# A hybrid diffusion backbone on one core: layer 1's attention-gate round of modulation weights moves to the last heads of layer 1, and modulation steps take two blocks of rows

## The chip, the cores and the metric

The kernel runs on one core of a Trainium2 chip. The metric is the device time of one execution in microseconds (us). Before the change three runs gave 1723.59, 1725.94 and 1725.95 us; the median is 1725.94 us. The engines named below are PE (TensorE, which multiplies matrices), DVE (VectorE), ACT (ScalarE), POOL (GpSimd) and SP (SyncE, which here issues the DMAs).

## The reference, cut to what matters

A two-layer transformer over 512 latent tokens and 256 context tokens, width 1024, all in fp32. Each layer is an attention part and a SwiGLU part, and each part is normalised, modulated, mixed, normalised again and added through a gate. Shift, scale and gate come from the conditioning vectors through one weight matrix per layer, `ada_w[l]` of 1024 x 6144:

```
mx = (silu(c) @ ada_w[l] + ada_b[l])         # 6 chunks of 1024; mc the same from c_ctx
hx = modulate(rmsnorm(x, g0), mx[0], mx[1])  # shift, scale of attention
yx = attention(hx, hc)                       # layer 0: window heads A and differential heads B; layer 1: MLA, 16 heads
x  = x + mx[2] * rmsnorm(yx, g1)             # gate of attention
hx = modulate(rmsnorm(x, g2), mx[3], mx[4])  # shift, scale of SwiGLU
x  = x + mx[5] * rmsnorm(swiglu(hx), g3)     # gate of SwiGLU
```

`ada_w` is 24 MB a layer and each of its elements is used once for two vectors, so it is a stream of loads with a few narrow matmuls behind each.

## The kernel before, in words

The kernel is written as one program for all engines. A scheduler places each engine's instructions in the order in which the code issues them, within what priorities and buffers allow; `tc.issue_after(x)` adds an order edge on PE alone. All DMAs are issued by SP on one queue (q1), in SP's order: a DMA whose buffer is not free yet holds up all DMAs behind it. Most products are made as three matmuls on a high and a low half of each operand, split by ACT (`wh`, `pth`) and DVE (`wl`, `ptl`, line 127).

**Modulation.** `ada_round(l, r, bank, sbt, ring)` (lines 252 to 286) is a Python generator that makes two of the six chunks of layer l: round r = 0 gives shift and scale of attention, r = 1 the gate of attention and the shift of SwiGLU, r = 2 the scale and the gate of SwiGLU. A round goes over 8 blocks of 128 rows. Each block issues two loads of 512 KB (`load`, line 204, tile `wst`, from `in_ada_w`) and, for each load, four matmuls at line 259 into the PSUM tile `ada`. Four matmuls of one load are called a **quad** here. The program's order lists a quad as `x4`; the trace counts two records for each fp32 matmul, so that there a quad is `x8`. After the eighth block the round copies the sums (line 265), transposes them (line 268, four of them), and adds and scales them on DVE (lines 273 to 286). Before the change the generator hands back control after each block, so a round is nine steps: eight blocks and the end. Whoever drives the generator decides where the next step stands in the order of PE; the loads go ahead as soon as the ring of `wst` buffers has a free one.

**Where the rounds stand.** Layer 0's rounds 0 and 1 come early, round 1 among the projections of queries and values (lines 557 to 571). In the differential heads (B, lines 856 to 892) one generator runs layer 0's round 2, then layer 1's rounds 0 and 1. The tables `FIRST` (head 0) and `ORDER` (heads 1 to 3) set at which point of a head each step stands: a letter `a` is one step, `f` transposes, `v` multiplies with values, and the bar splits what goes before and after a tile's softmax. The loads have a ring of 3 buffers, and of 4 once head 0 is two tiles in (`wst_a`). Rounds left over at the end of head 3 would be run out at `steps(ada, 99)`.

**Layer 1's heads** (M, lines 1545 to 1655): 16 heads, `HeadM`, each with scores (`scm`, line 1589), softmax (`p`, line 625), transposes (`tp`, line 639) and values (`pvm`, line 1607). The table `MORE` sets what else each head carries: `k` and `q` project the next pair's keys and queries and move them into place by DMA (`K<-K`, `K<-KR`, `Q<-Q`, `Q<-RQ`, line 133), `r` rotates, `u` makes values, `a` is one modulation step. Before the change heads 13, 14 and 15 carry three `a` each, all of layer 1's round 2, with the 3 buffers of the common ring `stage`. The attention gate of layer 1 is first used after the heads, in `out_proj(1)`.

Of the kernel before, what the change touches and what calls it, by code (L numbers as in the profile page):

```python
# [9 lines left out]
F32 = mybir.dt.float32  # L10
# [8 lines left out]
P = 128  # L19
# [96 lines left out]
def build(tc, d, cat, wat):  # L116
# [3 lines left out]
    def pool(stack, name, bufs=1, side="left", **kw):  # L120
        return stack.enter_context(tc.tile_pool(name=name, bufs=bufs, side=side, reuse_waits="tile", **kw))

    def psum(stack, name, side="left"):
        return stack.enter_context(tc.tile_pool(name=name, bufs=1, side=side, space=PSUM, reuse_waits="tile"))

    def sub(out, a, hi):
        nc.vector.tensor_sub(out, a, hi.bitcast(F32))  # L127
# [12 lines left out]
    wst = pool(top, "wst")  # L140
# [61 lines left out]
    def load(src, width, ring=None):  # L202
        st = (ring or stage).tile([P, 1024], F32, tag="wst", name="wst")
        nc.sync.dma_start(st[:, 0:width], src)
        return st[:, 0:width]
# [11 lines left out]
    def packed(name, ring=None):  # L217
        off, width = wat[name]
        return load(d["wpk"][off:off + P * width].rearrange("(p w) -> p w", p=P), width, ring)
# [32 lines left out]
    def ada_round(l, r, bank, sbt, ring=None):  # L252
        acc = bank()
        for k in range(NK):
            st = [load(d["ada_w"][l, k * P:(k + 1) * P, 2048 * r + 1024 * h:2048 * r + 1024 * h + 1024], 1024, ring)
                  for h in range(2)]
            for h in range(2):
                for q in range(4):
                    nc.tensor.matmul(acc[32 * q:32 * q + 32, 256 * h:256 * h + 256], scst[:, k, :],  # L259
                                     st[h][:, 256 * q:256 * q + 256],  # L260
                                     start=(k == 0 and h == 0), stop=(k == NK - 1 and h == 1),
                                     tile_position=(0, 32 * q), skip_group_check=True)
            yield
        sb = sbt()
        nc.vector.tensor_copy(sb, acc)
        tp = bank()
        for b in range(4):
            nc.tensor.transpose(tp[:, P * b:P * b + P], sb[:, P * b:P * b + P], ident)
        src = tp.rearrange("p (h e q r) -> p h q e r", h=2, e=2, q=4)
        dst = mods[l][:, 16 * r:16 * r + 16, :].rearrange("p (h q e) s -> p h q e s", h=2, q=4)  # L270
        bias = adab[:, l, 16 * r:16 * r + 16].rearrange("p (h q e) -> p h q e", h=2, q=4)
        for h in range(2):
            nc.vector.tensor_add(dst[:, h], src[:, h, :, :, 0:2], bias[:, h].unsqueeze(3).to_broadcast([P, 4, 2, 2]))

        def mk(out, chunk, gi, one):
            g = ng[:, l, gi, :].unsqueeze(2).to_broadcast([P, NK, 2])
            nc.vector.scalar_tensor_tensor(out, mods[l][:, 8 * chunk:8 * chunk + 8, :], one, g,
                                           op0=ALU.add, op1=ALU.mult)
        if r == 0:
            mk(amod[l][0], 1, 0, 1.0)  # L280
        elif r == 1:
            mk(ggc[l][0], 2, 1, 0.0)
        else:
            mk(amod[l][1], 4, 2, 1.0)
            mk(ggc[l][1], 5, 3, 0.0)
        yield

    def steps(gen, n):
        for _ in range(n):
            if next(gen, gen) is gen:  # L290
                break
# [136 lines left out]
    def blocks(name, scale=None):  # L428

        st = packed(name)  # L430
        w = st.shape[1] // 2
        res = []
        for j in range(2):
            h, l = (wring.tile([P, 512], F32R, tag=x, name=x)[:, 0:w] for x in ("wh", "wl"))
            a = st[:, w * j:w * j + w]
            if scale:
                nc.scalar.mul(h, a, scale)
                nc.vector.scalar_tensor_tensor(l, a, scale, h.bitcast(F32), op0=ALU.mult, op1=ALU.subtract)
            else:
                nc.scalar.copy(h, a)  # L440
                sub(l, a, h)
            res.append((h, l))
        return res
# [95 lines left out]
    def queries(i, w=None):  # L539
        big = yield from feat(w or blocks(f"q{i}", 0.125))  # L540
        rope(big[:, 0:NX], QO[:, i, 0:NX], tabs, 16, shift_tile())
        nc.scalar.copy(QO[:, i, NX:NT], big[:, NX:NT])

    def tok(t, src, slabs, width, n=NK):
# [7 lines left out]
        return lambda ps: mm3(lambda k: (src[0][:, k, P * t:P * t + P], src[1][:, k, P * t:P * t + P]), [(ps, mov)], n)  # L552

    ada = ada_round(0, 1, lambda: ps1.tile([P, 512], F32, tag="nt", name="ada"), shift_tile, ring_x)
    steps(keys(0, first[0]), 99)
    steps(queries(0, first[1]), 99)
    for i in range(1, 4):
        with tc.issue_after(ada_end):
            steps(ada, 1)
            steps(queries(i), 99)  # L560
    acc = [b[:, c:c + 384] for b in (bigs.tile([P, 1024], F32, tag="big", name="vps") for _ in range(2)) for c in (0, 512)]
    acc += [ps1.tile([P, 512], F32, tag="sm", name="vps")[:, 0:384] for _ in range(2)]
    for k in range(NK):
        steps(ada, 1)
        if k % 2 == 0:
            va = blocks(f"va{k // 2}")
        for t in range(6):
            for i, (a, b) in enumerate(((0, 0), (0, 1), (1, 0))):
                nc.tensor.matmul(acc[t], hT[a][:, k, P * t:P * t + P], va[k % 2][b],  # L569
                                 start=(k == 0 and i == 0), stop=(k == NK - 1 and i == 2))  # L570
# [285 lines left out]
    ps2 = PS2({"tp": (pstp, 2), "pv": (pst, 1), "ada": (pst, 1)})  # L856
    ptr = Ring((pb, 4))
    COMB = ((0, 1, 3), (3,))
    FIRST = ('v|t', 'w|a a', '|a', 'f0 a|f1 v0 f2', 'a|v1 a', 'a|a v2')
    ORDER = ("f3 a|f4 v3", "f5 v4|v5 a", "f6 a|v6 s", "f0 a|f1 v0", "|f2 v1 a", "|v2 a n")  # L860
    LAST = "f3 f4 v3 f5 v4 f6 v5 v6 s n"

    def run(word, new, old):
        for w in word.split():
            if w == "a":
                last = next(i for i in reversed(nc.cur_bb.bb.instructions) if i.engine == mybir.EngineType.PE)
                with tc.issue_after(last):
                    steps(ada, 1)
            elif w in "vtw":
                run_a(w, None, old)  # L870
            elif w == "s":
                old.squares()
            elif w == "n":
                old.norm(4, 6)
                old.norm(0, 4)
            else:
                x = new if w[1] in "012" else old
                (x.flip if w[0] == "f" else x.values)(int(w[1]))

    ring_a = Ring((wst, 3))  # L880
    ada = (x for l, r in ((0, 2), (1, 0), (1, 1))
           for x in ada_round(l, r, lambda: ps2.tile([P, 512], F32, tag="ada", name="ada"),
                              lambda: ring_a.slots[0][0].tile([P, 512], F32, tag="adasb", name="adasb", bufs=1), ring_a))
    qs = [stack(4, m, qring) for m in range(2)]
    for h in range(4):
        g = HeadB(h, qs)
        for t in range(6):
            a, b = (ORDER if h else FIRST)[t].split("|")
            g.scores(t, lambda: run(a, g, prev))
# [194 lines left out]
    class FfnWide:  # L1084
# [27 lines left out]
        def bank(self, tag):  # L1112

            return next(self.banks[tag]).tile([P, 512], F32, tag="b", name=tag)
# [329 lines left out]
    k = krT[:, 0:NX]  # L1444
# [25 lines left out]
    s_ma = ExitStack()  # L1470
# [74 lines left out]
    vp = pool(s_ma, "v1", bufs=2, side="right")  # L1545
    pp1 = pool(s_ma, "pp1", bufs=6, side="right")
    pt1 = pool(s_ma, "pt1", bufs=3, side="right")
    psb = PS(psum(s_ma, "ps_n"), {"sc": 2, "pv": 1, "tp": 2, "ada": 1})

    def mla_values(g):  # L1550
# [22 lines left out]
    def next_queries(p):  # L1573
        Q = yield from mla_queries(p, wp, psb.tile([P, 512], F32, tag="ada", name="qnps"), RQs[p // 2])
        KQ[p].append(Q)
        yield

    class HeadM:
# [21 lines left out]
        def values(self, j):  # L1600
# [15 lines left out]
    FIRST_M = "S0 u u S1 u u S2 u u f0 S3 x f1 x v0 f2 x v1"  # L1616
    LAST_M = "f3' v2' f4' v3' f5' v4' v5'"
    MORE = ("kkqqquu", "rrruuuu", "kkqqq", "rrr", "kkqqq", "uuuu", "kkqqq", "uurrr", "kkqqq", "uuuu", "kkqqq", "uu",
            "kkqqq", "aaa", "aaa", "aaa")
    V, RQs = {}, {0: RQ}  # L1620

    def chain(gens):
        for g in gens:
            yield from g
# [3 lines left out]
        "r": chain(next_rope(g) for g in range(1, 4)),  # L1628
        "k": chain(next_keys(p) for p in range(1, 8)),
        "q": chain(next_queries(p) for p in range(1, 8)),  # L1630
        "a": ada_round(1, 2, lambda: psb.tile([P, 512], F32, tag="ada", name="ada"), scratch),
    }
    prev = None

# [82 lines left out]
```

## Time and profile before

| what | value |
|---|---|
| median of three runs | 1725.94 us |
| the profiled execution | 1721.91 us, of which the span is 1720.1 us |
| granted TensorE clock, mean of the profiled execution | 0.983 of full speed (2.4 GHz) |
| busy share of the span | PE 95%, DVE 64%, ACT 51%, POOL 24% |
| heads B of layer 0 touched by the change | about 332 to 394 us |
| heads M that carry `a` | about 1237 to 1282 us; the last head ends about 1305 us |

The profile is one execution on the chip. Its page lists busy time of each engine, the span in 40 slices, the chain of work that ended last, and the costliest groups of instructions. The trace behind it can be asked for stretches (busy time of each engine, granted clock, share of DMA time), for waits, and for the instructions one after the other. An idle time is followed by `<-` and by what ended it.

### The profile page before, as it was taken

To read this page: it belongs to the slowest core of one execution; us is meant where nothing else is said; L and a number is where in the kernel's file an instruction comes from. 1 tells how busy PE (TensorE), PEld (TensorE's weight loads), DVE (VectorE), ACT (ScalarE), POOL (GpSimd) and SP (SyncE) were. 2 spreads that over 40 slices of the span, in tenths; PEclk is the share of its full clock that TensorE was granted. 3 is DMA by queue.
4 is the path that set the end of the run, shared out by engine and by line. 5 is a ranking of instruction groups with operands and counts; after the bars stand their busy time and mean duration, and the time that the engine had idled before them with its cause. 6 is when DMAs were issued, how large, how long until landed. Compare 5 with 4: busy or idle time off the path is not lost.

```text
span 1720.1 us, 27699 instructions
## 1 busy us (share of the span) xinstructions
PE 1630.9 (95%) x10274; PEld 1450.1 (84%) x10274; DVE 1095.1 (64%) x1924; ACT 882.8 (51%) x1888; POOL 420.9 (24%) x459
## 2 busy tenths in 40 slices
PE   6899999898979999999999997999999999999998
PEld 4688887667869999999888786899877899999886
DVE  3536888655676555555534866798766778777433
ACT  5325666554654444444333854676655745555332
POOL 2302434551212122221200112232220323332000
PEclk9999999999989999999999998999999999999999
DMA  9531214983323222222523432323463422333322
GB/s 361 188 110 36 63 46 132 258 282 125 109 75 99 72 66 72 98 74 74 210 97 135 163 125 66 81 61 94 101 196 115 144 97 101 99 114 105 102 98 86
DMA packets 61431, 203.35 MB, mean 118 GB/s; under 512 B 7280, under 2 KB 10480, under 8 KB 61296
## 3 DMA queue, kind: packets, MB, share of 16 engines
q1 hardware_dynamic: 61296, 201.58, 37.3%
q8 instruction: 81, 1.33, 0.3%
q14 instruction: 54, 0.44, 0.1%
HBM read 174.29 MB, written 10.49 MB: 107 GB/s over the span
## 4 chain that ended last, share of the span: by engine, by line
PE 79%; DMA 6%; DVE 6%; ACT 4%; issue 2%; POOL 1%; SPq 0%; DVEq 0%; POOLq 0%; ACTq 0%
PE A L1109 15%; PE y L1269 14%; PE C L1109 8%; PE y L230 6%; PE fps L230 6%; DMA wst<-in_ada_w 5%; PE B L1109 4%; PE scm L1589 3%; PE yc L1269 2%; PE tp L639 2%; PE pvm L1607 2%; PE vps L230 2%; PE ada L259 2%; PE vps L569 2%; DVE wl L127 1%
## 5 line engine op out<-in xcount | busy, mean ns | idle before, releaser
L127 DVE TENSOR_TENSOR wl<-wst,wh 128x512 fp32r<-128x512 f32 (+2 forms) x329 | 250.2, 768 | 201.5 <-ACT wh L1101 161.3
L1109 PE MATMUL A<-T,wh 128*128 128x384 f32 (+1 forms) x1280 | 278.9, 310 | 10.2 <-ACT T L936 7.8
L1101 ACT CAST wh<-wst 128x512 fp32r<-128x512 f32 (+1 forms) x266 | 161.8, 617 | 227.6 <-PE y L1269 120.5
L1109 PEld LDWEIGHTS A<-T,wh 128*128 128x128 f32 x1280 | 215.8, 191 | 11.8 <-ACT T L936 8.1
L1109 PE MATMUL A<-T,wl 128*128 128x384 f32 (+1 forms) x640 | 194.7, 310 | 1.0 <-DVE wl L127 1.0
L130 POOL TENSOR_SCALAR p<-p,sum 128x768 f32<-128x768 f32 (+2 forms) x96 | 83.4, 870 | 273.5 <-DVE sum L631 238.7
L1109 PE MATMUL C<-T,wh 128*128 128x384 f32 (+1 forms) x656 | 146.1, 312 | 2.4 <-ACT wh L1101 2.4
L1269 PE MATMUL y<-wl,ah 128*128 128x512 f32 x336 | 130.7, 389 | 0.0
L1269 PE MATMUL y<-wh,ah 128*128 128x512 f32 x336 | 130.4, 389 | 0.0
L1269 PE MATMUL y<-wh,al 128*128 128x512 f32 x336 | 130.4, 389 | 0.0
L1145 POOL TENSOR_TENSOR s<-wst 128x512 f32<-128x512 f32 x42 | 72.2, 1719 | 228.7 <-DMA wst<-in_wpk 167.0
L1101 ACT CAST wh<-S 128x512 fp32r<-128x512 f32 x126 | 73.3, 587 | 101.9 <-PE A L1109 48.5
L1109 PEld LDWEIGHTS A<-T,wl 128*128 128x128 f32 x640 | 121.3, 191 | 1.6 <-DVE wl L127 1.6
L1213 POOL TENSOR_TENSOR g<-g,E 128x384 f32<-128x384 f32 (+1 forms) x63 | 70.0, 1111 | 180.7 <-DVE E L1212 166.8
L1109 PEld LDWEIGHTS C<-T,wh 128*128 128x128 f32 x656 | 111.2, 191 | 2.9 <-ACT wh L1101 2.9
L230 PE MATMUL fps<-hT,wh 128*128 128x512 f32 (+1 forms) x416 | 98.0, 356 | 6.1 <-DVE KS L127 2.9
L1109 PE MATMUL C<-T,wl 128*128 128x384 f32 (+1 forms) x328 | 102.4, 312 | 0.1
L127 DVE TENSOR_TENSOR wl<-S,wh 128x512 fp32r<-128x512 f32 x126 | 85.8, 685 | 21.2 <-ACT wh L1101 20.4
L127 DVE TENSOR_TENSOR ptl<-tp,pth 128x512 fp32r<-128x512 f32 x124 | 84.3, 686 | 17.5 <-ACT pth L642 16.7
L642 ACT CAST pth<-tp 128x512 fp32r<-128x512 f32 x124 | 71.6, 585 | 38.2 <-PE tp L639 33.4
L1589 PE MATMUL scm<-K,Q 96*128 96x512 f32 (+1 forms) x384 | 83.1, 350 | 2.3 <-ACT p L625 1.3
L230 PEld LDWEIGHTS fps<-hT,wh 128*128 128x128 f32 x416 | 65.4, 194 | 19.8 <-PE sc L617 3.6
(390 smaller groups left out, 3985.1 us busy)
## 6 DMA issues: line engine op xcount, KB each, us to landing
wst<-in_wpk SPq DMA_DIRECT2D x107, 512.0 KB, 3.6
wst<-in_ada_w SPq DMA_DIRECT2D x96, 512.0 KB, 5.8
wst<-in_ffn_w SPq DMA_DIRECT2D x66, 512.0 KB, 3.5
xd<-xt SPq DMA_DIRECT2D x14, 512.0 KB, 2.6
xt<-xd SPq DMA_DIRECT2D x14, 512.0 KB, 5.1
xt<-in_x SPq DMA_DIRECT2D x8, 512.0 KB, 4.2
wst<-in_ab_w_out SPq DMA_DIRECT2D x8, 512.0 KB, 4.6
wst<-in_mla_w_out SPq DMA_DIRECT2D x8, 512.0 KB, 4.5
```

What stands on the lines that cost most here:

```text
L127: nc.vector.tensor_sub(out, a, hi.bitcast(F32))
L130: nc.gpsimd.tensor_scalar(out, a, s, 1.0, op0=ALU.mult, op1=ALU.mult)
L230: nc.tensor.matmul(ps, s, mov(k)[m], start=(k == 0 and i == 0), stop=(k == n - 1 and i == 2))
L259: nc.tensor.matmul(acc[32 * q:32 * q + 32, 256 * h:256 * h + 256], scst[:, k, :], st[h][:, 256 * q:256 * q + 256], start=(k == 0 and h == ...
L569: nc.tensor.matmul(acc[t], hT[a][:, k, P * t:P * t + P], va[k % 2][b], start=(k == 0 and i == 0), stop=(k == NK - 1 and i == 2))
L642: nc.scalar.copy(h, tp[:, 0:P * n])
L1101: nc.scalar.copy(h, src)
L1109: nc.tensor.matmul(ps, x, self.T.at(m, i, k), start=(start and k == 0 and j == 0), stop=(stop and k == 3 and j == 2), skip_group_check=True)
L1145: nc.gpsimd.tensor_sub(s3, a11, a21)
L1213: nc.gpsimd.tensor_mul(o, o, e)
L1269: nc.tensor.matmul(ys[t][j], a[x][:, P * place[t]:P * place[t] + P], w[j][y], start=(k == 0 and i == 0), stop=(k == NF - 1 and i == 2))
L1589: nc.tensor.matmul(ps[:, k0:k1], Q[0:96, e, a, P * i:P * i + P], K[0:96, e, b, k0:k1], start=(n == 0), stop=(n == 2))
```

## The change

It does four things.

1. `ada_round` hands back control after each second block: a round is four steps of two blocks (four quads, eight when nothing stands between) and one for the end.
2. In layer 0's round 1 the calls are fewer to match.
3. In the B heads round (1, 1) is dropped from the generator, and `FIRST` and `ORDER` have fewer `a`.
4. In the M heads the generator runs rounds (1, 1) and (1, 2), in ten steps (`aaaa`, `aaa`, `aaa`), with a ring of its own, `ring_m`: the 3 common buffers and 4 new ones (`wst_m`).

```diff
@@ ada_round
-            yield
+            if k % 2:
+                yield
@@ layer 0, round 1
     for i in range(1, 4):
         with tc.issue_after(ada_end):
-            steps(ada, 1)
+            if i > 1:
+                steps(ada, 1)
             steps(queries(i), 99)
...
     for k in range(NK):
-        steps(ada, 1)
         if k % 2 == 0:
+            if k:
+                steps(ada, 1)
             va = blocks(f"va{k // 2}")
@@ B heads
-    FIRST = ('v|t', 'w|a a', '|a', 'f0 a|f1 v0 f2', 'a|v1 a', 'a|a v2')
-    ORDER = ("f3 a|f4 v3", "f5 v4|v5 a", "f6 a|v6 s", "f0 a|f1 v0", "|f2 v1 a", "|v2 a n")
+    FIRST = ('v|t', 'w|a', '|', 'f0 a|f1 v0 f2', '|v1 a', '|a v2')
+    ORDER = ("f3|f4 v3", "f5 v4|v5 a", "f6|v6 s", "f0|f1 v0", "|f2 v1 a", "|v2 n")
...
-    ada = (x for l, r in ((0, 2), (1, 0), (1, 1))
+    ada = (x for l, r in ((0, 2), (1, 0))
@@ M heads
+    ring_m = Ring((wst, 3), (pool(s_ma, "wst_m", side="right"), 4))
...
-            "kkqqq", "aaa", "aaa", "aaa")
+            "kkqqq", "aaaa", "aaa", "aaa")
...
-        "a": ada_round(1, 2, lambda: psb.tile([P, 512], F32, tag="ada", name="ada"), scratch),
+        "a": chain(ada_round(1, r, lambda: psb.tile([P, 512], F32, tag="ada", name="ada"), scratch, ring_m) for r in (1, 2)),
```

How the instructions stand is seen in the order of an engine. PE, at the end of B head 2 and the start of head 3 (`sc<-KS` scores, `pvb` values, `rb` a small transpose of the norm, `tp` transposes of probabilities), before:

```order
L616 MATMUL sc_1315<-KS_470,qb 128x256
L617 MATMUL sc_1315<-KS_470,qb 128x256
L259 MATMUL ada<-wst,scst 32x256 x16
L616 MATMUL sc_1314<-KS_471,qa 128x512
L617 MATMUL sc_1314<-KS_471,qa 128x512
L616 MATMUL sc_1314<-KS_471,qa 128x256
L617 MATMUL sc_1314<-KS_471,qa 128x256
L639 MATMUL tp<-ident,p 128x128 x4
L794 MATMUL pvb<-pth,VB_467 128x256
```

and in the changed kernel at the same place:

```order
L619 MATMUL sc_1315<-KS_470,qb 128x256
L620 MATMUL sc_1315<-KS_470,qb 128x256
L642 MATMUL tp<-ident,p 128x128 x4
L619 MATMUL sc_1314<-KS_471,qa 128x512
L620 MATMUL sc_1314<-KS_471,qa 128x512
L619 MATMUL sc_1314<-KS_471,qa 128x256
L620 MATMUL sc_1314<-KS_471,qa 128x256
L642 MATMUL tp<-ident,p 128x128 x4
L797 MATMUL pvb<-pth,VB_467 128x256
```

The four quads between two scores are gone and the transposes follow the scores directly. From head 1's end to the end of head 3 PE has 28 quads in 23 pieces before; after, 12 in 5 pieces, and one set of four transposes less.

PE in the M heads, where two heads' work overlaps (`scm` scores, `pvm` values, `tp` transposes), before:

```order
L1607 MATMUL pvm<-ptl,V 128x256 x2
L639 MATMUL tp<-ident,p 128x128 x4
L259 MATMUL ada<-wst,scst 32x256 x6
L1589 MATMUL scm<-K,Q 128x512
L1589 MATMUL scm<-K,Q 128x256
L1589 MATMUL scm<-K,Q 128x512
L1589 MATMUL scm<-K,Q 128x256
L1589 MATMUL scm<-K,Q 128x512
L1589 MATMUL scm<-K,Q 128x256
L259 MATMUL ada<-wst,scst 32x256
L639 MATMUL tp<-ident,p 128x128 x4
L259 MATMUL ada<-wst,scst 32x256 x3
```

and in the changed kernel:

```order
L1611 MATMUL pvm<-ptl,V 128x256 x2
L642 MATMUL tp<-ident,p 128x128 x4
L259 MATMUL ada<-wst,scst 32x256 x8
L642 MATMUL tp<-ident,p 128x128 x4
L259 MATMUL ada<-wst,scst 32x256 x4
L1593 MATMUL scm<-K,Q 128x512
L1593 MATMUL scm<-K,Q 128x256
L1593 MATMUL scm<-K,Q 128x512
L1593 MATMUL scm<-K,Q 128x256
L1593 MATMUL scm<-K,Q 128x512
L1593 MATMUL scm<-K,Q 128x256
L259 MATMUL ada<-wst,scst 32x256 x4
```

The quads stand closer together: 32 of them in 27 pieces over heads 13 to 15, where there were 16 in 15 pieces, and two sets of transposes, the second of which stands with the end of head 15.

SP at the start of the M heads (`wst<-in_wpk` weights of keys and queries, `K` and `Q` the moves of the second pair's context part into place):

```order
 L133 DMA Q<-RQ 32x1024 x2
+L204 DMA wst<-in_ada_w 128x1024
 L204 DMA wst<-in_wpk 128x512
 L204 DMA wst<-in_wpk 128x384
+L133 DMA K<-K 64x2x256
 L204 DMA wst<-in_wpk 128x256
-L133 DMA K<-K 64x2x256
+L204 DMA wst<-in_ada_w 128x1024 x3
 L133 DMA K<-KR 32x2x256 x2
```

Four of the moved loads are issued here, some 160 us before the heads that use them, three of them directly ahead of the move `K<-KR`. These four go to the new buffers. The first three that the steps need go to the common buffers and stand among the moves of the last pairs, and the other 25 of the 32 loads follow there.

## Rows read from the trace of the kernel before

**Rows 1.** The page: the chain that ended last, by engine and line.

```profile
PE 79%; DMA 6%; DVE 6%; ACT 4%; issue 2%; POOL 1%; SPq 0%; DVEq 0%; POOLq 0%; ACTq 0%
PE A L1109 15%; PE y L1269 14%; PE C L1109 8%; PE y L230 6%; PE fps L230 6%; DMA wst<-in_ada_w 5%; PE B L1109 4%; PE scm L1589 3%; PE yc L1269 2%; PE tp L639 2%; PE pvm L1607 2%; PE vps L230 2%; PE ada L259 2%; PE vps L569 2%; DVE wl L127 1%
```

**Rows 2.** Stretches of B heads, of M heads, of the start: busy us of each engine.

```profile
core 0: us, PE busy (x) PEld busy (x) DVE busy (x) ACT busy (x) POOL busy (x), PEclk, DMA share, GB/s
304.30:334.00 29.70, 26.00 (x216) 18.60 (x217) 18.66 (x35) 16.64 (x39) 18.67 (x20) 0.94 0.85 250
334.00:365.90 31.90, 28.75 (x267) 20.22 (x265) 19.33 (x39) 17.57 (x43) 17.45 (x22) 1.00 0.92 276
365.90:391.70 25.80, 25.62 (x228) 18.77 (x225) 15.61 (x28) 14.07 (x34) 12.25 (x15) 1.00 0.73 247
332.00:394.50 62.50, 58.93 (x526) 42.54 (x526) 39.72 (x77) 34.70 (x81) 31.79 (x39) 1.00 0.82 258
1237.60:1282.00 44.40, 42.77 (x339) 30.51 (x338) 26.96 (x52) 21.91 (x46) 9.98 (x11) 1.00 0.82 230
1282.00:1305.00 23.00, 21.19 (x161) 19.22 (x160) 18.62 (x34) 16.20 (x33) 5.44 (x6) 1.00 0.01 4
16.00:48.00 32.00, 27.18 (x224) 14.70 (x216) 14.80 (x27) 13.51 (x23) 8.00 (x11) 0.89 1.03 388
```

**Rows 3.** The same view, of line 259 alone: PE busy, PEld busy, clock.

```profile
332.00:394.50 62.50, 17.90 (x232) 5.31 (x232) 1.00 0.82 258
1237.60:1282.00 44.40, 12.04 (x128) 3.33 (x128) 1.00 0.82 230
```

**Rows 4.** PE's waits, 332 to 394.5 us: total us, times, longest.

```profile
PE ada L259 <- DMA wst<-in_ada_w: 3.1, 4, 1.3
```

**Rows 5.** PE's waits, 1237 to 1282 us.

```profile
PE ada L259 <- DMA wst<-in_ada_w: 1.6, 2, 1.4
```

**Rows 6.** PE's timeline in B heads 2 and 3: start, us, instruction.

```profile
352.65 0.64 PE L259 MATMUL ada<-wst,scst 128*32 128x256 f32 x8
353.22 0.50 PE L616 MATMUL sc<-KS,qa 128*128 128x512 f32 x1
...
361.81 0.60 PE L268 MATMUL ada<-ident,adasb 128*128 128x128 f32 x4
362.17 0.36 PE L794 MATMUL pvb<-ptl,VB 128*128 128x256 f32 x1
...
364.05 1.93 PE L259 MATMUL ada<-wst,scst 128*32 128x256 f32 x32
365.91 0.50 PE L616 MATMUL sc<-KS,qa 128*128 128x512 f32 x1
```

**Rows 7.** The loads of `ada_w` (L204), 1239 to 1272 us: issue, time to landing.

```profile
L204 SPq DMA_DIRECT2D wst<-in_ada_w x13: 327/328/1517, 1239.6 to 1270.8; - x13
DMA to landing us min/median/max: 3.8/5.1/8.3
```

**Rows 8.** PE's timeline at the start of the M heads.

```profile
1079.57 1.81 PE L1589 MATMUL scm<-K,Q 96*128 96x256 f32 x10
...
1084.86 1.32 PE L1589 MATMUL scm<-K,Q 96*128 96x512 f32 x6 [1.33 <-ACT p L625]
```

**Rows 9.** The moves `K<-KR` (L133): first 1076 to 1078 us, then 1252 to 1254 us.

```profile
L133 SPq DMA_DIRECT2D K<-KR x2: 593/608/622, 1076.4 to 1077.1; - x2
DMA to landing us min/median/max: 2.0/2.0/2.0
...
L133 SPq DMA_DIRECT2D K<-KR x2: 517/550/582, 1252.5 to 1253.1; - x2
DMA to landing us min/median/max: 4.2/4.4/4.5
```

**Rows 10.** PE's timeline near the end of the M heads.

```profile
1298.32 0.60 PE L639 MATMUL tp<-ident,p 128*128 128x128 f32 x4
1299.38 0.66 PE L639 MATMUL tp<-ident,p 128*128 128x128 f32 x4 [0.45 <-DVE ptl L127]
```

## The prediction

> **What bounds the kernel now.** The chain of waits says where a saved microsecond counts. PE has 79% of it, DMA has 6%, and 5% are the loads of `ada_w` alone [rows 1]: the kernel is bound by PE's own work, and the modulation loads are the one transfer that the end waits for in earnest. A modulation matmul thus costs its full time on PE wherever PE is full, and moving it from one full place to another gains nothing by itself. What can be gained is waiting: for the loads that come too late where the rounds stand now, and for another chain for which a quad fills a gap.
>
> So the second view is the busy time by stretch. In B heads 2 and 3 PE is busy 28.75 of 31.90 us and 25.62 of 25.80, in the M heads with `a` 42.77 of 44.40, in the last M head 21.19 of 23.00 [rows 2]. Both places are PE-bound, and both are short of DMA: the DMA share is 0.92 in head 2 and 0.82 in the M heads, against 1.03 at 388 GB/s at the start of the kernel, and 0.01 in the last head. The third view, PE's waits, shows what that costs: 3.1 us in four waits in the B heads [rows 4] and 1.6 us in two in the M heads [rows 5], all for `wst<-in_ada_w`.
>
> I make the sum on the profiled execution, 1721.91 us. It lies 4.0 us under the median of the three runs, 1725.94 us, and I put the difference that I find on the median. The runs lie 0.14% apart, and less than 0.2% (3.45 us) I take for no change that can be told.
>
> **What a quad costs.** A single quad starts at 352.65 us and the next instruction at 353.22, so 0.57 us; four together run from 364.05 to 365.91, 1.86 us [rows 6]. So each further quad of a piece costs (1.86 - 0.57) / 3 = 0.43 us, and a piece 0.14 us more. Line 259 is busy 17.90 us in the B stretch with 232 records, that is 29 quads [rows 3]. By the order they stand in 24 pieces: (17.90 - 29 x 0.43) / 24 = 0.23 us a piece. In the M stretch 12.04 us for 16 quads in 15 pieces gives (12.04 - 6.88) / 15 = 0.34 us. I take 0.23 and 0.34, which have the neighbours' share in them, over 0.14.
>
> **B heads, what goes.** 13 quads in 6 pieces are left there: 13 x 0.43 + 6 x 0.23 = 7.0 us, so 10.9 us of PE's work go. Four transposes go, 0.36 us by the start of the next instruction [rows 6], and the load waits, 3.1 us [rows 4], since half the loads are gone and the ring of four runs ahead. Together -14.4 us.
>
> **B heads, what comes.** Without the quads PE may wait for the softmax chain instead. Per head PE had 25.6 to 28.8 us of work; with 10.9 us gone over two and a half heads that is some 22 to 24 us. DVE has 15.6 to 19.3 us, ACT 14.1 to 17.6, POOL 12.3 to 18.7 [rows 2]: none becomes the bound by its sum, but they follow each other within a tile, and in head 1, where POOL has 18.67 us, PE is busy only 26.00 of 29.70. A grouped step also asks for four loads at once, and the second pair may not have landed. Neither wait can be read before it exists. Its lower bound is nothing; its upper, that heads 2 and 3 get as idle as head 1, 12% of some 47 us, 5.9 us. I take 1.5 us, nearer to nothing, because head 3 has PE full to 25.62 of 25.80 with the order the same. B: -12.9 us.
>
> **M heads, quads.** 32 quads in 27 pieces instead of 16 in 15: 32 x 0.43 + 27 x 0.34 = 22.9 us against 12.04, so +10.9 us, and four transposes, +0.36. Nothing hides it: PE is full there. The waits of 1.6 us [rows 5] should go, as seven loads are ahead when the first step comes, and I leave 0.3 of them: -1.3. At the end, copy, transposes and adds of round 2 stand with head 15, where each tile is a chain of transposes, ACT and DVE and PE waits 0.45 us for `ptl` at a time [rows 10]; DVE is busy 18.62 of 23.00 us there [rows 2], and gets about a microsecond more, part of it on that chain: +0.5 (0 to 1). M heads: +10.5 us.
>
> **M heads, loads.** Thirteen loads issue from 1239.6 to 1270.8 us and the last lands 3.9 us on [rows 7], 35 / 13 = 2.7 us each with three buffers; at 388 GB/s one takes 1.35 us. After the seven that are ahead, 25 must land while PE does some 56 us of work (44.4 + 10.9, and a little of the last head): they keep up below 56 / 25 = 2.2 us each. In B head 2, with four buffers, DMA moved 276 GB/s, 1.9 us for a load. With seven buffers I expect less than that, so nothing is added. The moves of the last pairs stand between these loads, where K and Q are wanted a head later; their place costs nothing as long as the loads keep up.
>
> **Start of the M heads.** Before, `K<-KR` of the second pair is issued at 1076.4 and 1077.1 us and lands 2.0 us later [rows 9], and the ten scores that need it start at 1079.57, at once behind other work [rows 8]: a slack of about half a microsecond to one. Now three loads of 512 KB are issued directly ahead of it, at 388 GB/s 4.0 us, of which part runs while SP still waits. The softmax that follows is already late by 1.33 us [rows 8], so a late score is passed on. By the row behind loads, 4.2 to 4.5 us to landing [rows 9], the move is 2.4 late, less the slack, 1.5; by the whole 4.0 us and the weights of the next queries behind the first load, 5. With nothing lost where PE finds other work: 0.5. I take 2.0 us, near the row of the same move behind loads.
>
> The Trainium skill (DMA: Bandwidth & Descriptors, section Queues, rings and completion order) says that a DMA engine takes the descriptors of one ring in order and turns between queue rows packet by packet. By the first half the move waits for all of the three loads that still run, and the sum has its 2 us or more; had the loads another queue row, by the second half, the move would pass between them and the sum would be about 2 us less. The 2.0 us against 4.2 to 4.5 [rows 9] agree with the first.
>
> **Layer 0, round 1.** One quad moves some rows down and two join two others; SP's order is the same. Two pieces fewer: -0.2 us by the 0.14 above, or nothing.
>
> **Sum.** -12.9 + 10.5 + 2.0 - 0.2 = -0.6 us. 1721.91 becomes 1721.3, and on the median 1725.94 - 0.6 = 1725.3 us: within 0.2%. The two rounds' 10.9 us cancel to the tenth, so that the time is decided by the waits alone: 3.1 + 1.3 that go, against 4.0 that come.
>
> **Rivals.** First, **the new waits don't come**: the B gain is whole (-14.4), the start of the M heads costs 0.5, the tail nothing: -14.4 + 10.0 + 0.5 - 0.2 = -4.1 us, 1721.8 us, and 1720 where a wait behind the loads' 5% of the chain [rows 1] goes too. For it speaks that the scheduler fills PE from two heads at a time. Chance 0.35, on the faster side.
>
> Second, **the M heads become bound by their loads**. If they stay at the 2.7 us each of rows 7, because the same queue has the K and Q moves and the buffers are freed by matmuls only just in time, 25 x 2.7 = 67.5 us are needed for 56: +11.5, and the net is -0.6 + 11.5 = +10.9, 1737 us. It decides from 2.2 us a load on. Against it speaks that 2.7 us was with three buffers and 5.1 us from issue to landing, so that three in flight give 5.1 / 3 = 1.7 us each, and the buffers were waiting to be freed by PE, not for the bus. Chance 0.10.
>
> Third, **the B heads turn to the softmax chain** and the start of M costs its upper bound: a wait of 5.9 us instead of 1.5 gives +3.8 us, and 1729; with 5 us at the start, 1732. Chance 0.10.
>
> Last, **the grouping does nothing of what it says**: by the order the pieces of M are still 27 for 32 quads, so the step of two blocks is pulled apart by the scheduler, and of its saving only the five pieces in B are real. That is in the sum already.
>
> **How the numbers follow.** The forecast, within 0.2%, has 0.45, the first rival 0.35, the second 0.10, the third 0.10. The third lies on either side of +3.45, mostly over it, and the first's lower part is under -3.45: faster 0.34, same 0.46, slower 0.20. The forecast's own range is 1722.5 to 1729. The range for 8 in 10 reaches down to the first rival's lower end with half a microsecond for the runs' own spread, and a little less, 1718.5, and up to the third's 1732, leaving out the second.
>
> **What would show it.** Right: no `ada` wait in the B heads after head 1, heads 2 and 3 shorter by some 13 us, heads 13 to 15 longer by some 10, ten `scm` at the start of M with an idle time ahead of them that ends with `K<-KR`. Wrong: an `ada` wait of microseconds in heads 14 and 15 (second rival), PE idle for `p`, `cf` or `ptl` in B heads 2 and 3 of over 3 us (third), or no idle time at the start of M (first).

## The result and the profile after

The changed kernel took 1735.07 us (median of four runs, 1734.87 to 1739.32) against 1725.66 us before: a ratio of 1.0058, 95% interval 1.0037 to 1.0079. Run again beside later experiments, it took 1737.71 us against 1725.24 us, 1.0067 (1.0049 to 1.0086). The forecast was 1725.3 us, no change that can be told, with a range up to 1732. By the two ratios the kernel became slower by some 10 to 12 us, and the time lies above the range.

The profiled execution took 1735.00 us with a span of 1733.2 us; that of before had 1720.1 us. The page's chain answers to [rows 1]:

```profile
PE 80%; DVE 6%; DMA 5%; ACT 4%; issue 2%; POOL 1%; SPq 0%; DVEq 0%; POOLq 0%; ACTq 0%
PE A L1112 16%; PE y L1272 14%; PE C L1112 8%; PE fps L230 6%; PE y L230 6%; PE B L1112 4%; DMA wst<-in_ada_w 3%; PE scm L1593 3%; PE tp L642 3%; PE pvm L1611 2%; PE yc L1272 2%; PE ada L259 2%; PE vps L230 2%; PE vps L572 1%; PE sc L619 1%
```

The loads of `ada_w` lost their place in the chain only in part (3% instead of 5%), and PE still carries four fifths. Where the time went is read from the stages. The table is worked out from start times: of the first `pvb` and the first `A` matmul (B heads to the first matmul of layer 0's SwiGLU), and of the first `scm` and the first `dps` matmul (M heads to the tail of layer 1's projection).

| stage, us | before | after | difference |
|---|---|---|---|
| first `pvb` to first `A` | 485.6 - 298.1 = 187.5 | 483.2 - 297.7 = 185.5 | -2.0 |
| first `A` to first `scm` | 1073.1 - 485.6 = 587.5 | 1070.1 - 483.2 = 586.9 | -0.6 |
| first `scm` to first `dps` | 1355.8 - 1073.1 = 282.7 | 1369.2 - 1070.1 = 299.1 | +16.4 |

The forecast had -12.9 for the first line and +12.5 for the third. Most of the error is in the B heads. These are the waits of PE there, from 334 to 425 us (waiting matmul and what it waited for: total us, times, longest), after:

```profile
PE ada L259 <- DMA wst<-in_ada_w: 3.9, 2, 3.4
PE pvb L797 <- ACT pth L645: 2.2, 1, 2.2
PE rb L817 <- POOL tiny L812: 1.9, 1, 1.9
PE sc L619 <- ACT p L628: 1.4, 2, 0.8
PE pvb L797 <- DVE ptl L127: 0.8, 1, 0.8
PE tp L642 <- DVE QO L819: 0.7, 1, 0.7
```

In the kernel before, the same stretch has the 3.1 us of [rows 4], 0.2 us for `ptl` and two waits behind the heads, 5.6 us in all:

```profile
PE y L230 <- ACT oh L1009: 1.3, 1, 1.3
PE y L230 <- ACT p L625: 0.9, 1, 0.9
```

After, it is 10.9 us, and two kinds of wait make it. The waits for loads have not gone: with half the loads there is still 3.9 us of waiting, 3.4 of it in one piece. And five lines are new or (`ptl`) longer, 7.0 us together, all on the softmax and norm of heads 2 and 3. The stretch around the long wait (columns as in [rows 2]) and its instructions:

```profile
341.00:346.00 5.00, 1.72 (x25) 0.57 (x24) 1.03 (x3) 1.76 (x6) 3.61 (x4) 1.00 1.04 228
346.00:350.00 4.00, 3.34 (x17) 2.36 (x18) 0.70 (x1) 0.00 (x0) 0.48 (x1) 0.60 1.00 343
```

```profile
342.63 0.64 PE L259 MATMUL ada<-wst,scst 128*32 128x256 f32 x8 [0.55 <-DMA wst<-in_ada_w]
...
346.66 1.02 PE L259 MATMUL ada<-wst,scst 128*32 128x256 f32 x8 [3.39 <-DMA wst<-in_ada_w]
```

A quad that takes 0.64 us at 342.63 takes 1.02 us at 346.66: after 3.39 us of idling the granted clock is 0.60 on average over the next 4 us, that is, mostly at the lower level of 1.2 GHz. The DMA engines are busy all through that wait (share 1.04, at 228 GB/s): the load that PE waits for was issued at 333.9 us and took 12.7 us to land, behind other loads and the moves of `qa`. The clock falls behind the other two long waits too, `pth` (2.2 us) and `tiny` (1.9 us):

```profile
345.00:355.00 10.00, 8.34 (x51) 6.79 (x51) 3.75 (x7) 3.61 (x9) 3.19 (x4) 0.83 0.61 202
...
385.00:395.00 10.00, 7.09 (x31) 5.46 (x31) 9.94 (x20) 7.94 (x16) 3.42 (x6) 0.83 0.47 159
...
415.00:425.00 10.00, 8.13 (x42) 6.58 (x40) 3.09 (x9) 3.89 (x11) 1.33 (x1) 0.83 0.00 1
```

Three stretches of 10 us at a mean clock of 0.83, each (1 - 0.83) x 10 = 1.7 us of full-speed work lost. The kernel before has one such stretch there, 395 to 405 us. So in this trace the waits of 3.39, 2.22 and 1.87 us cost 1.7 us each on top of themselves, and the forecast had no term for it. This is not a fixed price: in the kernel before the longest wait ahead of its stretch is 1.3 us, and in the trace of e1 (below) 20 us around one wait of 3.3 us run at a mean clock of 0.66, (1 - 0.66) x 20 = 6.8 us of work lost:

```profile
345.00:365.00 20.00, 17.11 (x99) 14.24 (x102) 7.64 (x14) 6.63 (x15) 7.77 (x8) 0.66 0.44 123
```

The Trainium skill (TensorE: Matmul & The Clock Gate, section Part 1: The HAM clock gate) says that the clock has these two levels and that they follow how busy PE has been; the rows agree.

The M heads, same view, and line 259 alone (answers to [rows 2, 3]):

```profile
1237.00:1312.00 75.00, 23.46 (x256) 7.76 (x256) 1.00 0.71 222
```

23.46 us of PE for 32 quads, where 22.9 were forecast, and there is no wait for a load in heads 13 to 15 at all. That part went as expected. The start of the M heads did not:

```profile
1080.68 3.33 PE L1593 MATMUL scm<-K,Q 96*128 96x256 f32 x10 [3.27 <-DMA K<-KR]
```

```profile
L133 SPq DMA_DIRECT2D K<-KR x2: 597/610/622, 1075.6 to 1076.2; - x2
...
DMA to landing us min/median/max: 4.8/4.9/5.0
```

The ten scores that began at once in [rows 8] wait 3.27 us, because the move takes 4.8 to 5.0 us instead of 2.0 ([rows 9]); and they then take 3.33 us instead of 1.81, at half the clock. The last of the three loads ahead of it, issued at 1073.2 us, landed 7.0 us later, at 1080.2; the move, issued at 1075.6, at 1080.5. By the Trainium skill (DMA: Bandwidth & Descriptors, section Queues, rings and completion order) the descriptors of one ring are consumed in order; the trace agrees, with 0.3 us between the two landings.

### The profile page after: what moved, and what is told of

Same layout as the page of the kernel before. It is cut to its first block, busy times and chain, and to the rows that moved or that the text cites. A ratio compares the mean times of both kernels' runs of the same rounds, so it can differ in the third digit from the quotient of the medians.

```text
span 1733.2 us, 27702 instructions
## 1 busy us (share of the span) xinstructions
PE 1639.0 (95%) x10274; PEld 1457.6 (84%) x10274; DVE 1096.4 (63%) x1924; ACT 884.8 (51%) x1888; POOL 422.1 (24%) x459
## 4 chain that ended last, share of the span: by engine, by line
PE 80%; DVE 6%; DMA 5%; ACT 4%; issue 2%; POOL 1%; SPq 0%; DVEq 0%; POOLq 0%; ACTq 0%
PE A L1112 16%; PE y L1272 14%; PE C L1112 8%; PE fps L230 6%; PE y L230 6%; PE B L1112 4%; DMA wst<-in_ada_w 3%; PE scm L1593 3%; PE tp L642 3%; PE pvm L1611 2%; PE yc L1272 2%; PE ada L259 2%; PE vps L230 2%; PE vps L572 1%; PE sc L619 1%
## 5 line engine op out<-in xcount | busy, mean ns | idle before, releaser
L1112 PE MATMUL B<-T,wh 128*128 128x384 f32 (+1 forms) x352 | 81.7, 314 | 0.9 <-DVE g L1207 0.8
```

Of the source, the lines that this page charges most:

```text
L1112: nc.tensor.matmul(ps, x, self.T.at(m, i, k), start=(start and k == 0 and j == 0), stop=(stop and k == 3 and j == 2), skip_group_check=True)
```

## The experiments

Each kernel is named by its label; a ratio is against the kernel before on the same chip, with its 95% interval, and "x us" behind it is that ratio taken of 1726 us. The kernel before and the changed kernel were run again among them. The experiments lie on four chips, and the runs of one kernel spread by some 10 us (before, over all chips: 1720.8 to 1734.9), so kernels are compared by their ratios, and differences under 3 us are not read from the medians. "The B stage" is the first line of the table above.

**The two halves apart.** In e1_b_only:

```diff
-        "a": chain(ada_round(1, r, ..., scratch, ring_m) for r in (1, 2)),
+        "a": ada_round(1, 2, ..., scratch, None, 1),
+    nc.vector.memset(mods[1][:, 16:32, :], 0.0)
+    nc.vector.memset(ggc[1][0], 0.0)
```

> The B half alone: round (1,1) is left out of the B heads as in the changed kernel and is computed nowhere (its gate and shift are set to zero once), and the M heads are those of before (round (1,2) in one-block steps with three buffers). Theory A, each place pays by itself, and the B heads cannot use the freed PE time because the softmax chain and the grouped loads take its place: 2 to 4 us faster than before, some 1722 to 1724 us. Theory B, the forecast's gain in the B heads is real and all of the loss is made in the M heads: 13 us faster than before, some 1713 us.

Measured: 1718.67 us, 0.9944 (0.9920 to 0.9968), -9.7 us, between the two theories and nearer to neither. In e2_m_only the B heads are those of before, with their tables and one-block steps, and the M heads those of the changed kernel:

```diff
-    ada = (x for l, r in ((0, 2), (1, 0))
+    ada = (x for l, r in ((0, 2), (1, 0), (1, 1))
```

> The M half alone: the B heads have the tables, one-block steps and all three rounds of before, and the M heads compute round (1,1) a second time as in the changed kernel, with the seven-buffer ring. Theory A: the M heads cost 11.4 us and the start of the M heads 5 us, together 16 us slower than before, some 1742 us. Theory B: 22 us slower, some 1748 us. If the start of M is an accident of the schedule and not of the early loads: 11 to 12 us slower, 1737 us.

Measured: 1739.57 us, 1.0076 (1.0050 to 1.0102), +13.1 us. In its trace other work stands ahead of the ten scores: they still wait 2.22 us for `K<-KR`, but run at full clock (1.90 us), and the 41st score matmul starts 28.2 us after the first, where it is 26.8 in the kernel before and 32.1 in the changed one. First `scm` to first `dps` is 294.1 us, +11.4. The halves add up to +3.4 us, with about 6 us of uncertainty; the change measured +10 to +12. Some 4 us of what is missing is the start of the M heads, which e2 has only in part; the rest isn't settled.

**The start of the M heads.** Two kernels keep the loads away from it. e4_m_ring3 has only the common buffers:

```diff
-    ring_m = Ring((wst, 3), (pool(s_ma, "wst_m", side="right"), 4))
-        "a": chain(ada_round(1, r, ..., scratch, ring_m) for r in (1, 2)),
+        "a": chain(ada_round(1, r, ..., scratch) for r in (1, 2)),
```

> The changed kernel with the three common buffers for the loads of the M heads, so that no load can be issued at the start of M. Theory A, the early loads make the wait of 3.3 us for K<-KR and the half clock behind it: the start of M gives back 5 us; then the loads are late, at 1.7 us each (5.1 us in flight, three buffers) 32 of them take 54 us and PE waits up to 4 us: 1730 to 1734 us. At 2.7 us each they take 86 us and PE waits some 25 us: 1755 us.

Measured: 1731.20 us, 1.0033 (1.0017 to 1.0050), +5.7 us. e6_m_gate keeps all seven buffers and holds the first seven loads back:

```diff
+        if gate and ring is not None:
+            nc.vector.tensor_copy(st[:, 0:1], gate.pop())
...
+        if h == 13:
+            gate.extend([OT[:, 4, 0:1]] * 7)
```

> The changed kernel with the first seven loads of the M heads held back until head 13: a one-column copy of heads 8 and 9's output into the buffer is written ahead of each, so that no load stands at the start of M; all else is as in the changed kernel. Theory A, the early loads cost the start of M 5 us (wait for K<-KR 3.3 us and the half clock behind it): 1730 us, no idle time of over 1 us before the ten context scores. Rival, the start of M is late for another reason, or the seven loads in a row at head 13 cost as much: 1734 to 1736 us.

Measured: 1730.59 us, 1.0032 (1.0018 to 1.0047), +5.5 us. PE's waits from 1055 to 1080 us in its trace:

```profile
PE ltp L1399 <- DVE nh L1394: 2.1, 1, 2.1
PE scm L1597 <- ACT p L632: 1.3, 1, 1.3
PE early L234 <- ACT kvT L1407: 1.2, 1, 1.2
PE scm L1597 <- DVE K L127: 0.9, 1, 0.9
```

No wait for `K<-KR`, and the ten scores take 1.81 us again. Both kernels give back 4 to 6 us, as theory A had it. In their traces the 41st score matmul starts 27.0 us after the first, as in the kernel before. So the early loads are the cause: the price is 5 us, not the 2 of the forecast. e4 also shows that three buffers nearly carry the M heads: in its trace the loads of the M heads make PE wait 2.8 us in all, in three waits. The second rival, 2.7 us a load, is out.

**The B heads: grouping or place.** e3_b_single undoes the grouping: the generator hands back control after each block, and the tables are those of before, so that the quads stand early:

```diff
-    FIRST = ('v|t', 'w|a', '|', 'f0 a|f1 v0 f2', '|v1 a', '|a v2')
-    ORDER = ("f3|f4 v3", "f5 v4|v5 a", "f6|v6 s", "f0|f1 v0", "|f2 v1 a", "|v2 n")
+    FIRST = ('v|t', 'w|a a', '|a', 'f0 a|f1 v0 f2', 'a|v1 a', 'a|a v2')
+    ORDER = ("f3 a|f4 v3", "f5 v4|v5 a", "f6 a|v6 s", "f0 a|f1 v0", "|f2 v1 a", "|v2 a n")
```

> The changed kernel with one-block steps in the B heads (the tables FIRST and ORDER of before, two rounds, done by the middle of head 2). Theory A1, the lost gain in B is the wait for grouped loads (2.7, 0.6 and 3.4 us) and the half-clock stretch behind it: 4 to 6 us faster than the changed kernel, 1729 to 1731 us. Theory A2, it is the softmax chain that ends last in heads 2 and 3 whatever the loads do: within 1.5 us of the changed kernel, 1734 to 1736 us, with more idle time before p, pth and ptl in head 3.

Measured: 1738.21 us, 1.0066 (1.0042 to 1.0090): no better than the changed kernel, and the B stage of its trace is 188.3 us. One-block steps alone are not the cure: with two loads a step and the same four buffers PE waits as long for loads as with grouped steps, from 304 to 425 us (7.3 and 7.7 us in the two traces of the changed kernel):

```profile
PE ada L259 <- DMA wst<-in_ada_w: 7.9, 6, 4.8
```

SP waits for buffers in both. These are its waits for a quad to free one, from 320 to 350 us, in e3, in the changed kernel and in the kernel before, in this order:

```profile
SPq L204 <- PE ada L259: 15.6, 8, 5.7
SPq L204 <- PE ada L259: 15.6, 7, 5.7
SPq L204 <- PE ada L259: 11.6, 9, 5.5
```

The longest, 5.5 to 5.7 us, is there whatever the size of the step. Then the changed kernel was run once more:

> The changed kernel once more, beside the other kernels on one chip and with a second trace. All theories: 1735 us, +/- 3. What the second trace is for: theory A says that B heads 2 and 3 again wait for the fourth load of a grouped step and for ACT, DVE and POOL, with a half-clock stretch behind each wait of 2 us or more; if the B heads of the first trace were a bad draw, heads 2 and 3 end 4 us or more earlier.

Its B stage took 485.8 - 297.5 = 188.3 us, 2.8 more than in the first trace; the waits for `pth`, `tiny`, `p` and `ptl` are the same to 0.1 us, and the load waits are one of 2.9 us. And the kernel before:

> The kernel before once more, for a second trace. Its first profiled execution took 1721.9 us, near the lowest of all its runs (1720.8 to 1734.9), and the B heads of the changed kernel differ by up to 9 us between traces of the same code. Theory A: the second trace shows the same waits in the same places (for loads in heads 1 and 2, none for p, pth or the norm's POOL result in head 3), and the B heads end 2 to 5 us later than in the first. If the first trace was typical: within 1 us.

It took 1725.65 us, 0.9994 (0.9981 to 1.0008), and the B stage of its trace 488.4 - 298.2 = 190.2 us. So the first trace of before was 2.7 us shorter there than the second, as theory A had it. All traces with the B heads of before (the two, and e2) have 187.5, 190.2 and 190.0 us; the seven with those of the changed kernel have 185.5, 188.3 (e5), 188.1 (e1), 188.9 (e4), 179.0 (e6), 185.0 (e7) and 182.3 (e8). The means are 189.2 and 185.3: the B heads gave some 4 us in the traces, where e1's runs say 5.5 to 13.8 for the half alone. What the seven differ by is the loads, 4.2 to 8.5 us of waiting from 304 to 425 us, and the clock, 0.91 to 0.97 from 304 to 420 us; the waits of the chain are in all of them.

With these traces the forecast's miss in the B heads can be divided, as an estimate. All waits of PE from 304 to 425 us are 9.4, 12.0 and 9.9 us with the B heads of before and 13.5 to 16.1 us with those of the changed kernel, on the mean 10.4 and 14.7: +4.3, where the forecast had -3.1 + 1.5 = -1.6. Of the 10.4 us the loads have 7.5, of the 14.7 they have 6.6: hardly less, and the chain has come on top. The clock is 0.97, 0.97 and 0.94 with the B heads of before, and its mean falls from 0.961 to 0.934, 0.027 x 116 = 3.1 us. So 5.9 + 3.1 = 9.0 us are missing, and -12.9 + 9.0 = -3.9 is what the means of the stage show.

e10_b_none takes another round out of the B heads:

```diff
-    ada = (x for l, r in ((0, 2), (1, 0))
+    ada = (x for l, r in ((0, 2),)
```

> The B half carried further: rounds (1,0) and (1,1) are both left out (the weights that they would make are constants set once), so that only layer 0's round 2 stands in the B heads, in heads 0 and 1; the M heads are those of before. Theory A, without quads the B heads are held by the softmax chain: of the further 7 us of PE's work at most 2 to 5 us become time, beside the load waits that go: 1710 to 1716 us. Theory B, PE's work and the load waits alone set the time: 7 us of work and 5 us of waits go, 1706 us or less.

Measured: 1708.39 us, 0.9887 (0.9870 to 0.9903), some 10 us under e1; the B stage 174.5 us. By the ratio, taken of 1726 us, that is 1706.5 us; the median itself lies between the two theories, so it is nearer to theory B, if to either. The chain does not hold the heads in a hard way, since a further round still brings about its PE time, though the chain's waits grow (`pth` 2.3, `p` 2.2, `ptl` 2.2 us). My theory A1/A2 split was too coarse, and the next two kernels settle it. e11_b_spread has the work of the changed kernel in one-block steps that go down to head 3:

```diff
+    FIRST = ('v|t', 'w|a', '|a', 'f0|f1 v0 f2', 'a|v1', 'a|v2')
+    ORDER = ("f3|f4 v3 a", "f5 v4|v5 a", "f6|v6 s a", "f0|f1 v0 a", "|f2 v1 a", "|v2 n")
```

> The changed kernel with the two rounds of the B heads in one-block steps, four in head 0 and five in each of heads 1 to 3 (in the changed kernel: two-block steps, three and two a head), so that quads stand in head 3 too, where PE waits for the softmax chain. Theory A, PE's idle time in head 3 is what the removed round filled: quads placed there fill it again, the waits of 2.2, 1.9, 1.4 and 1.2 us shrink, and the loads of heads 1 and 2 have more time: 4 to 7 us faster than the changed kernel, 1729 to 1732 us. Rival, only the sum of PE's work counts: 1735 us.

Measured: 1728.69 us, 1.0008 (0.9997 to 1.0019), 6 to 10 us faster than the changed kernel; the B stage of its trace is 473.9 - 297.8 = 176.1 us. PE's waits from 334 to 425 us:

```profile
PE y L230 <- DVE xn L354: 2.0, 1, 2.0
PE y L230 <- ACT oh L1012: 1.4, 1, 1.4
PE y L230 <- ACT p L628: 0.9, 1, 0.9
PE pvb L797 <- DVE ptl L127: 0.8, 2, 0.5
PE sc L619 <- ACT p L628: 0.7, 3, 0.3
PE tp L642 <- DVE QO L819: 0.5, 1, 0.5
```

No wait for a load is left here (2.6 us from 304 us on), and the waits for `pth` and `tiny` are gone; those of `y` stand behind the heads and two of them are in before too. The clock tells the same. Over 304 to 420 us of this kernel (columns as in [rows 2]) it is 0.99:

```profile
304.00:420.00 116.00, 105.32 (x774) 83.71 (x775) 75.48 (x136) 69.02 (x157) 57.42 (x64) 0.99 0.55 172
```

and in e5, the changed kernel, 0.91:

```profile
304.00:420.00 116.00, 102.74 (x708) 82.45 (x706) 69.51 (x120) 62.31 (x137) 52.15 (x60) 0.91 0.57 168
```

0.08 x 116 = 9.3 us of full-speed work lie between these two clocks alone; e5 is at the lower end of the seven traces, which go up to 0.97. e13_b_ring7 keeps the two-block steps and their places and gives the loads three more buffers:

```diff
-                ring_a.slots = Ring((pool(s_q, "wst_a"), 4)).slots
+                ring_a.slots = Ring((pool(s_q, "wst_a"), 4), (wst, 3)).slots
```

> The changed kernel with seven buffers instead of four for the loads of the B heads (the common three behind the four); the two-block steps and their places stay. Theory A1, the loads: a two-block step uses all four buffers, so the next step's loads cannot be issued before it runs; with three more ahead the waits of 0.6 and 3.4 us in head 2 and the half clock behind them go: 4 to 6 us faster than the changed kernel, 1729 to 1731 us. Theory A2, the chain of head 3: the waits for ACT, DVE and POOL (together 7 us) stay as they are and the time is within 2 us of the changed kernel, 1734 to 1737 us.

Measured: 1728.06 us, 1.0011 (0.9997 to 1.0024), as fast as the spread. PE's waits, 300 to 425 us:

```profile
PE pvb L797 <- ACT pth L645: 2.6, 2, 2.2
PE sc L619 <- ACT p L628: 2.3, 6, 0.8
PE y L230 <- DVE xn L354: 2.0, 1, 2.0
PE rb L817 <- POOL tiny L812: 1.9, 1, 1.9
PE ada L259 <- DMA wst<-in_ada_w: 1.8, 1, 1.8
PE pvb L797 <- DVE ptl L127: 1.1, 2, 0.8
```

The load waits shrink from 7.7 us (e5, the same stretch) to 1.8 in one piece, the chain's waits stay or grow, the B stage is 477.0 - 297.6 = 179.4 us, and the time falls by 7 to 10 us. The stage of one trace alone would not show it, since e6 has 179.0 us with four buffers; the medians do. The sizes agree, as an estimate: 6.6 - 1.8 = 4.8 us less waiting than the mean of the seven, and at a clock of 0.97 from 304 to 420 us instead of 0.934 another 0.036 x 116 = 4.2 us. So A1 holds for the buffers: four are too few for these loads in these places, the load that comes last is waited for, and the clock falls behind the wait. That it is the step of two blocks that makes them too few is not shown; e3, with one-block steps at early places, waits as long, and e11, with one-block steps spread out, does not. The chain's 7 us are real as well, but e13 has them and is as fast as e11, which has 2 us of them: they seem to cost less than they show.

**A better place.** PE of the kernel before waits at the start of layer 1 for the norms of the latent queries (from 1030 to 1100 us, kernel before):

```profile
PE ltp L1392 <- DVE ln L1387: 5.9, 3, 2.9
PE ltp L1392 <- DVE nh L1387: 2.1, 1, 2.1
```

Round (1,1) was put there, two one-block steps behind each of the four norms, with the B heads of the changed kernel and the M heads of before; e7_front_3 has three buffers for it and e8_front_5 five.

```diff
         lat_T(t, pss[t], col("qg"), qT, 3, 0, scratch, "c")
+        steps(ada11, 2)
```

> Round (1,1) is computed in neither the B heads nor the M heads but between the norms of the latent queries at the start of layer 1, where PE of the kernel before waits 2.9, 2.4, 2.1 and 1.2 us for DVE and ACT, with the three common buffers; the B heads are those of the changed kernel, the M heads those of before. Theory A, what the round costs is decided by whether PE waits where it stands: the B gain of some 8 us (median of the B half alone) stays, and the round costs 0 to 4 us: 1719 to 1722 us. Rival, the loads of three buffers hold up the weights behind them on the queue: the start of M is 6 us or more later, 1725 us or more.

> The same with five buffers (two new ones) for the round at the start of layer 1. Theory A: 1 to 2 us faster than with three, 1717 to 1721 us, since two more loads are ahead when the waits begin. Rival as there.

Measured for the two: 1734.46 us, 1.0052 (1.0034 to 1.0070), and 1722.09 us, 0.9979 (0.9965 to 0.9993). With three buffers the rival is right: quads wait 8.6 us for loads and the weights behind them come late. With five the time is 1 us above the range of theory A: the waits for `ln` and `nh` are gone, and 3.0 us of load waits and 3.5 us for a late `Q<-RQ` stand in their place. The spread B heads with this place are e12_spread_front:

> The same B heads, with round (1,1) in the waits at the start of layer 1 (five buffers) and the M heads of before. Theory A, rounds cost least where PE waits anyway: the gains of this placing (3 to 4 us against before) and of the spread B heads add up, 1714 to 1718 us. Rival: 1722 us as without the spread.

Measured: 1713.72 us, 0.9924 (0.9910 to 0.9938), 13 us faster than before and over 20 faster than the changed kernel: the gains add up, as theory A had it. e14_joined adds seven gated buffers for round (1,2) in the M heads:

> The kernel with spread B heads and round (1,1) at the start of layer 1, and in addition seven buffers for round (1,2) in the M heads, held back until head 13 so that none is loaded early. Theory A: the M heads' load waits of 1.6 us go and nothing else changes: 1 to 2 us faster than without, 1712 us, under both kernels. Rival: the seven loads in a row at head 13 hold up the moves of the last pairs: 1714 us or more.

Measured: 1712.56 us, 0.9927 (0.9906 to 0.9948), the same as without: the rival's time is not reached, and the gain of theory A is within what the runs spread. From 1200 to 1320 us no quad of its trace waits for a load. But in the trace of e12, with three buffers, those waits are only 0.5 us, where theory A counted on the 1.6 us of the kernel before: there was little left to gain.

## Why the prediction was wrong, point by point

- **What bounds the kernel.** Right: PE's own work and the loads. Right too was that moving the 10.9 us from one full place to another gains nothing and that the waits decide. The waits were counted wrongly.
- **The price of a quad.** Right: 22.9 us forecast for the M heads, 23.46 measured; in the B heads 16 quads less took 24.96 - 15.21 = 9.8 us of PE away (line 259, 300 to 420 us), where 10.9 were forecast. That grouping saves time by itself is not shown: e3 without it is as slow as the changed kernel.
- **B heads, what goes.** This is the step that failed: "the load waits, 3.1 us, since half the loads are gone and the ring of four runs ahead". Half the loads are gone, but the ring of four does not run ahead: SP waits up to 5.7 us for a free buffer, and PE's load waits fall only from 7.5 to 6.6 us in the mean of the traces. With three more buffers they are 1.8 us, and 7 to 10 us of time come back (e13).
- **B heads, what comes.** The second half of the same step. I had named the grouped step and the chain as possible waits and put both at 1.5 us. The chain alone, the third rival's mechanism, has 7.0 us of waits for ACT, DVE and POOL in heads 2 and 3, above the bound of 5.9. I took 1.5 "because head 3 has PE full to 25.62 of 25.80 with the order the same", but head 3 was full because its quads filled it. e11 puts quads back there and these waits shrink to about 2 us in the heads.
- **The clock.** No term of the sum held it. Stretches at half speed cost some 3 us more in the B heads than with the B heads of before, by the estimate above, and 1.5 us in the ten scores at the start of the M heads.
- **Start of the M heads.** The mechanism was right and the size was off: 5.3 us (the 41st score matmul starts 32.1 us after the first, 26.8 before), forecast 2.0, and just over the upper bound of 5. Half speed behind the wait is the missing part, 3.33 us instead of 1.81 for the ten scores.
- **M heads, loads and tail.** Right: no load wait in heads 13 to 15. The M heads after the start cost 267.0 - 255.8 = 11.2 us against 10.5.
- **The trace as a base.** The profiled execution of before was 4 us under the median. The second one (e9) took 2.9 us more, and has 2.7 us of that in the B stage. The forecast put its difference on the median as if every stage of that execution had been typical.

The rivals: of the second nothing was seen; the first would have needed the new waits not to come; the third, 1729 to 1732 us at a chance of 0.10 (its sums give 1729.7 and 1732.7), described both places and fell short by 3 us, because it named the chain and left out the load waits that stay and the half clock.

## What to carry to other kernels

Fewer loads do not end the waits for loads while the ring stays as short: where PE waits for a load and the issuing engine has waited for a free buffer before it (here up to 5.7 us, with steps of one block and of two), give the ring more buffers, or place the quads further apart, before counting the wait as gone. Filler matmuls are worth their place, not only their time: put them where PE waits for another engine's chain (here 0.9927 and 0.9924 of the time before), not where PE is full, and leave some at each point whose chain they cover. New buffers let the scheduler load as early as they are free, also ahead of a small move on the same queue that someone waits for; e6 shows that holding such loads back costs one small instruction each.

## What the runs showed of the hardware that was not expected

Waits of PE of 1.9 to 3.4 us were followed by matmuls at half speed (a quad 1.02 us instead of 0.64, ten scores 3.33 instead of 1.81), so that a wait cost 1.5 to 1.7 us more than the waits view says in the trace of the changed kernel, and 6.8 us more in one place of e1. Not every such wait had this price. The clock is 1.00 around the 2.22 us for `K<-KR` in e2 (1084 to 1092 us), and around 2.0 us for `xn` in the changed kernel (425 to 435 us):

```profile
1084.00:1092.00 8.00, 5.78 (x38) 4.85 (x37) 4.71 (x8) 4.68 (x10) 0.92 (x1) 1.00 0.48 106
425.00:435.00 10.00, 8.04 (x37) 6.59 (x36) 5.95 (x10) 5.08 (x16) 2.80 (x6) 1.00 0.31 105
```

And the time of the same code in one stage spread by 10 us between traces (B stage 179.0 us in e6, 188.9 in e4, with the same B heads): with it go the load waits, 4.2 and 8.5 us, and the clock from 304 to 420 us, 0.97 and 0.91. Which execution gets which was not settled.
